# Seven-product gate and up for the last twelve tiles of two more FFN halves, with RWKV emitted at 2.5 steps

## The chip, the cores and the metric

The kernel runs on one core of one Trainium2 chip. The metric is the device time of one execution in microseconds; before the change it is 2428.38 us, the median of three runs (2426.93 to 2428.75). Five engines work side by side, each through its own instructions in a fixed order: TensorE (PE, with its weight loads PEld), VectorE (DVE), ScalarE (ACT), GpSimd (POOL) and SyncE (SP), which here issues the DMAs. [...]

## The reference

A decoder trunk on a sequence of 1024 tokens of width 1024, in float32. Two layers, each a mixer and a SwiGLU FFN with residual additions, and a final RMSNorm. Layer 0 mixes with causal pooling and a Mamba-2 SSD, layer 1 with RWKV-7 and an RG-LRU.

```python
for layer in range(DEPTH):                      # DEPTH = 2
    hn = rmsnorm(h, mix_norm_g[layer])
    h = h + (even_mixer if layer % 2 == 0 else odd_mixer)(hn, ...)
    hn = rmsnorm(h, ffn_norm_g[layer])
    h = h + swiglu(hn, ffn_w_gate[layer], ffn_w_up[layer], ffn_w_down[layer])
return rmsnorm(h, final_norm_g)

def swiglu(h, w_gate, w_up, w_down):            # 1024 -> 2816 -> 1024
    return (silu(h @ w_gate) * (h @ w_up)) @ w_down
```

RWKV is a recurrence over the tokens; the kernel computes it in chunks of 64 tokens, each of which needs the state that the chunk before it leaves.

## The kernel before

**Layout.** Activations lie transposed, features on the 128 partitions and tokens along the free axis. The tokens are worked in two halves of 512, so there are four FFN calls: (half, layer) = (0,0), (1,0), (0,1), (1,1). Every matrix product takes three matmuls for one (high part by high part, high by low, low by high, lines 370 to 372): each weight block arrives by DMA as a `raw` tile, ACT rounds it to its high part `whi` (line 348), DVE subtracts that to get the low part `wlo` (line 349), and so for the activations.

**Plain FFN.** `ffn` (line 478) works on pairs of 128-wide tiles of the 2816 hidden features: 22 tiles, 11 pairs. `gate_up` runs gate and then up through `dense`, with 48 matmuls of 512 columns for each tile; `down` multiplies a group of pairs by the down weights and adds into `h`. `GROUPS` gives the groups. `dense` yields after each block of four k tiles, 24 matmuls; such a stretch is called a main step below. A plain FFN has 72 of them, some with half the matmuls.

**Seven-product FFN.** The last call, (1,1), uses `stras_ffn` (line 667). For each tile the eight block products of gate and up with the token halves are replaced by seven (Strassen-Winograd): 84 matmuls of 256 columns, lines 663 to 665. It needs sums of the activations (`t1` to `t4`, made in `stras_norm`, line 590, from the normalized tiles, 16 persistent tiles of the tag `m`) and sums of the weights, which `stras_weights` (line 622) makes on DVE for every tile, with the splits into high and low. Four finished tiles are multiplied by the down weights in `down`.

**Order of the work.** The program is emitted by Python generators. `Side` and `weave` put RWKV (`rwkv`, about 63 steps) beside the FFN that does not depend on it: after each main step `RATES["rw"]` = 1.4 RWKV steps are emitted. The framework's scheduler then orders the instructions of each engine: earlier emission has the higher priority, and an instruction that is not ready is passed by later ones that are. On the engine that order is fixed. Buffers are tagged: a pool has a number of buffers for each tag, `m` has 28 (`BUFS`), `raw` 3, `whi` and `wlo` 4 each, `m4` 2. RWKV's 512-column tiles are all of the tag `m`.

In layer 1 the order is: FFN (1,0) with RWKV of half 0 beside it; `outproj` of half 0, and the input projection `in1` of half 1; FFN (0,1) with RWKV of half 1, where the weave stops at main step `LIMIT` = 58 to let `outproj` of half 1 run, with `stras_norm` inside the last pair; then the pool `oq` is closed, `sp` opened, and FFN (1,1) runs in seven products.

**Lines that the prediction follows.** RWKV first makes its per-chunk operands (lines 1203 to 1332: decays, scaled keys, `ps_A` products in line 1305, a triangular inverse `X` in lines 1327 and 1329, with trips through DRAM), then the chain of eight chunks: `chain1` (line 1408, matmul with the state `S`), an ACT copy (1410), `chain2` (1418), a DVE copy (1419), `chain3` (1429), two DVE operations that make the next state (1434, 1435). `gn` normalizes every second chunk (lines 1481 to 1508); its last tile is `ro`, line 1508. RWKV's output goes to DRAM and is read by `outproj`.

Of the kernel before, what the change touches and what calls it, by code (L numbers as in the profile page):

```python
# [5 lines left out]
F32 = mybir.dt.float32  # L6
# [80 lines left out]
class Trunk:  # L87
# [390 lines left out]
    def ffn(self, hf, layer, h, hn, nxt=None, r=None):  # L478
# [48 lines left out]

        pair = 0
# [61 lines left out]
    def stras_norm(self, X, h, r, gname, goff):  # L590


        nc = self.nc
        for k in range(4):
            f, s = [], []
            for j in (k, k + 4):
                hn = self.dp.tile([P, H], F32, name="hn", tag="tf", bufs=BUFS["tf"])
                nc.vector.scalar_tensor_tensor(hn, h[j], self.pv(gname, goff + j), r(), op0=MULT, op1=MULT)
                hl = self.hn_tiles(j)
                self.split(hn, *hl)  # L600
                f.append(hn)
                s.append(hl)
                if j < 4:
                    yield
            (b11, b12), (b21, b22) = [(x[:, :256], x[:, 256:]) for x in f]
            lo = [self.op.tile([P, H], F32R, name="tl", tag="m", bufs=BUFS["m"]) for _ in range(2)]
            hi = [self.op.tile([P, H], F32R, name="th", tag="m", bufs=BUFS["m"]) for _ in range(2)]
            ts = [self.m2("ts") for _ in range(2)]
            t1, t2, t3, t4 = [x[:, q * 256:(q + 1) * 256] for x in ts for q in range(2)]
            nc.vector.tensor_tensor(t1, b12, b11, op=SUB)  # L610
            nc.vector.tensor_tensor(t2, b22, t1, op=SUB)
            nc.vector.tensor_tensor(t3, b22, b12, op=SUB)
            nc.vector.tensor_tensor(t4, b21, t2, op=SUB)
            for q in range(2):
                self.split(ts[q], hi[q], lo[q])
            L, R = slice(0, 256), slice(256, 512)
            for b, (x, c) in dict(b11=(s[0], L), b21=(s[1], L), b22=(s[1], R), t1=((hi[0], lo[0]), L), t2=((hi[0], lo[0]), R),
                                  t3=((hi[1], lo[1]), L), t4=((hi[1], lo[1]), R)).items():
                X.setdefault(b, []).append([y[:, c] for y in x])
            yield  # L620

    def stras_weights(self, f, wg, wu):
# [16 lines left out]
        def one(src, pool, tag, bufs):  # L639
            hl = [pool.tile([P, 512], F32R, name=x, tag=tag, bufs=bufs) for x in ("wbh", "wbl")]  # L640
            self.split(src, *hl)
            return hl
# [3 lines left out]
        W["a22"] = one(a22, *((self.dp, "nrb", 2) if f % 2 else (self.dp, "h", BUFS["h"])))  # L646
# [5 lines left out]
        W["s2"] = one(a11, self.op, "m", BUFS["m"])  # L652
        nc.vector.tensor_tensor(a12, a12, a11, op=SUB)
        W["s4"] = one(a12, self.op, "m", BUFS["m"])
# [12 lines left out]
    def stras_ffn(self, hf, layer, h, X):  # L667
# [4 lines left out]
        acts = []  # L672

        def finish(e):
# [5 lines left out]
            if n % 8 < 5:  # L680
                hl = self.act_tiles()
            else:
                hl = [self.dp.tile([P, H], F32R, name=x, tag="h", bufs=BUFS["h"]) for x in ("acth", "actl")]
# [3 lines left out]
        def down(base, act):  # L687
            for m in range(4):
                pp = [self.psum("py"), self.psum("py")]
                for _ in self.dense(wd, base, len(act), m * 256, 256, act, pp):  # L690
                    pass
                for t in range(2):
                    nc.vector.tensor_tensor(h[2 * m + t], h[2 * m + t], pp[t], op=ADD)
                yield

        prev = None
        todo = None
        for n in range(NFF):
            W = self.stras_weights(n, wg, wu)
            Y, Z = self.pd("py1"), self.pd("pz1")  # L700
            self.stras_mm(Y[:, L], W["a11"], X["b11"], True)
            rr = self.dp.tile([P, H], F32, name="rr", tag="st", bufs=BUFS["st"])
            nc.scalar.copy(rr[:, L], Y[:, L])
            self.stras_mm(Z[:, R], W["s1"], X["t1"], True)
            c22 = self.dp.tile([P, H], F32, name="c22", tag="tf", bufs=BUFS["tf"])[:, :256]
            nc.scalar.copy(c22, Z[:, R])
            if prev:
                finish(prev)
            self.stras_mm(Y[:, L], W["s2"], X["t2"], False)
            nc.scalar.copy(rr[:, R], Y[:, L])  # L710
            self.stras_mm(Z[:, L], W["a12"], X["b21"], False)
            self.stras_mm(Z[:, R], W["s4"], X["b22"], False)
            g = self.dp.tile([P, H], F32, name="sg", tag="sg", bufs=BUFS["sg"])
            nc.vector.tensor_tensor(g, rr, Z, op=ADD)
            th = self.dp.tile([P, H], F32, name="th", tag="tf", bufs=BUFS["tf"])
            nc.scalar.activation(th, g, AF.Tanh, scale=0.5)
            nc.vector.scalar_tensor_tensor(g, th, 1.0, g, op0=ADD, op1=MULT)
            self.stras_mm(Y[:, L], W["s3"], X["t3"], False)
            nc.vector.tensor_tensor(c22, c22, Y[:, L], op=ADD)
            prev = (Y, W, g, c22, n)  # L720
            yield
            if n % 4 == 0 and n:
                todo = down(n - 4, acts[-4:])
            if todo:
                next(todo)
                yield
        finish(prev)
        yield from todo
        yield from self.ffn_final(hf, wd, NFF - 2, acts[-2:], h)
# [842 lines left out]
RATES = dict(o0=0.5, b0=4, ssd0=1.75, ssd1=1.0, rw=1.4)  # L1572
LIMIT = 58


def trunk(tc, ins, out):
    with ExitStack() as stack:
# [42 lines left out]
        with tc.tile_pool(name="op", bufs=1) as op, ExitStack() as late:  # L1620
            t.odd_open(op, late.enter_context(tc.tile_pool(name="oq", bufs=1)))
# [3 lines left out]
            side = Side(t.rwkv(0, sA))  # L1625
            st = weave(t.ffn(1, 0, hB, hn2), side, RATES["rw"])
            side.finish()
# [12 lines left out]
            side = Side(t.rwkv(1, sB))  # L1640
            hB = []
            hn = []
            X = {}
            f = t.ffn(0, 1, hA, hn2, t.stras_norm(X, hB, lambda: R["B"], "ffn_norm_g", 8))
            weave(f, side, RATES["rw"], LIMIT)
            side.finish()
            stB = run_all(t.outproj(1, 1, wo1, t.yd[1], hB, t.hn2, lambda: t.m2("hB")))
            t.later(2, lambda: rstd("B", stB))
# [33 lines left out]
```

## Time and profile before

| what | value |
|---|---|
| median of three runs | 2428.38 us |
| the profiled execution, device time | 2427.69 us |
| its span, first to last instruction | 2425.9 us |
| PE, PEld, DVE busy | 2373.9, 1986.4, 1656.8 us |
| ACT, POOL busy | 966.5, 244.0 us |
| mean granted TensorE clock | 0.992 of full speed |
| first gate matmul of FFN (1,0) | 909.0 us |
| first matmul of `outproj` of half 0 in layer 1 | 1370.0 us |
| first matmul of FFN (1,1) | 2068.7 us |

The shares are of the whole span; what a change in one stage is worth is read from that stage. A matmul's duration in the profile includes its way through the pipeline, so that consecutive ones overlap: the pace of a stream is read from how many start in a window, not from the mean duration.

### The profile page before, as it was taken

How to read it: one execution, taken by the hardware profiler on the slowest of the kernel's cores; microseconds unless marked ns; L12 is line 12 of the kernel's file. 1: busy time of each engine (PE TensorE's matmuls, PEld its weight loads, DVE VectorE, ACT ScalarE, POOL GpSimd, SP SyncE). 2: the span in 40 equal slices, each digit the busy share in tenths (PEclk: the TensorE clock that was granted, in tenths of full speed). 3: DMA queues.
4: the chain of work that ended last, by engine and by line, in shares of the span. 5: the costliest groups of instructions: out<-in, count | busy, mean ns of one | idle time of the engine just before them, and what ended most of it. 6: DMA issues, size and time to landing. Idle time of an engine off the chain costs nothing.

```text
span 2425.9 us, 34902 instructions
## 1 busy us (share of the span) xinstructions
PE 2373.9 (98%) x13115; PEld 1986.4 (82%) x13115; DVE 1656.8 (68%) x3248; ACT 966.5 (40%) x1708; POOL 244.0 (10%) x231
## 2 busy tenths in 40 slices
PE   7989999999999999999999999999999999899998
PEld 6878887888878887788888888877888887899997
DVE  7878767764476675775565668676656548887775
ACT  4444433322234555233333346442333334454442
POOL 2131121211112010100000111010000000000000
PEclk9999999999999999999999999999999999899999
DMA  5433533333245333644324443335433442333332
GB/s 165 120 91 103 158 112 103 89 111 98 83 135 178 88 117 88 167 132 123 99 78 141 145 133 94 109 114 158 136 103 91 117 140 83 122 113 105 103 103 73
DMA packets 318874, 280.28 MB, mean 116 GB/s; under 512 B 46067, under 2 KB 296073, under 8 KB 318705
## 3 DMA queue, kind: packets, MB, share of 16 engines
q1 hardware_dynamic: 317872, 277.64, 39.0%
q8 instruction: 103, 1.69, 0.3%
q0 software_dynamic: 832, 0.41, 0.1%
q14 instruction: 67, 0.54, 0.1%
HBM read 247.51 MB, written 30.49 MB: 115 GB/s over the span
## 4 chain that ended last, share of the span: by engine, by line
PE 91%; DVE 4%; DMA 2%; issue 1%; SPq 1%; ACT 1%; POOL 0%; DVEq 0%; ACTq 0%; POOLq 0%
PE py L370 6%; PE py L371 6%; PE py L372 6%; PE pg L371 5%; PE pg L372 5%; PE pg L370 5%; PE pu L370 5%; PE pu L371 5%; PE pu L372 5%; PE pi L370 4%; PE pi L371 4%; PE pi L372 4%; PE po L370 2%; PE po L371 2%; PE po L372 2%; PE py L663 2%
## 5 line engine op out<-in xcount | busy, mean ns | idle before, releaser
L348 ACT CAST whi<-raw 128x512 fp32r<-128x512 f32 (+1 forms) x664 | 407.6, 619 | 877.8 <-PE pu L371 207.9
L349 DVE TENSOR_TENSOR wlo<-raw,whi 128x512 fp32r<-128x512 f32 (+1 forms) x664 | 477.6, 723 | 401.5 <-ACT whi L348 394.7
L371 PE MATMUL py<-actl,whi 128*128 128x512 f32 x672 | 266.8, 397 | 0.0
L370 PE MATMUL py<-acth,whi 128*128 128x512 f32 x672 | 264.0, 401 | 1.4 <-DVE sg L510 0.5
L372 PE MATMUL py<-acth,wlo 128*128 128x512 f32 x672 | 264.9, 395 | 0.0
L370 PE MATMUL pu<-hnh,whi 128*128 128x512 f32 x560 | 223.5, 400 | 0.0
L371 PE MATMUL pu<-hnl,whi 128*128 128x512 f32 x560 | 223.1, 398 | 0.0
L372 PE MATMUL pu<-hnh,wlo 128*128 128x512 f32 x560 | 222.2, 397 | 0.0
L370 PE MATMUL pg<-hnh,whi 128*128 128x512 f32 x528 | 211.2, 400 | 0.0
L371 PE MATMUL pg<-hnl,whi 128*128 128x512 f32 x528 | 209.3, 396 | 0.0
L372 PE MATMUL pg<-hnh,wlo 128*128 128x512 f32 x528 | 208.4, 396 | 0.0
L370 PE MATMUL pi<-hnh,whi 128*128 128x512 f32 x512 | 204.4, 399 | 0.1
L371 PE MATMUL pi<-hnl,whi 128*128 128x512 f32 x512 | 203.2, 397 | 0.0
L372 PE MATMUL pi<-hnh,wlo 128*128 128x512 f32 x512 | 201.7, 396 | 0.0
L370 PEld LDWEIGHTS py<-acth,whi 128*128 128x128 f32 x672 | 126.9, 189 | 31.3 <-issue 1.5
L372 PEld LDWEIGHTS py<-acth,wlo 128*128 128x128 f32 x672 | 127.1, 189 | 29.1
L371 PEld LDWEIGHTS py<-actl,whi 128*128 128x128 f32 x672 | 127.1, 189 | 27.3 <-DVE actl L236 0.2
L522 DVE TENSOR_TENSOR h<-h,py 128x512 f32<-128x512 f32 x160 | 107.6, 682 | 34.9 <-PE py L372 33.8
L370 PEld LDWEIGHTS pu<-hnh,whi 128*128 128x128 f32 x560 | 105.3, 188 | 25.4 <-issue 2.2
L372 PEld LDWEIGHTS pu<-hnh,wlo 128*128 128x128 f32 x560 | 105.4, 188 | 24.4 <-issue 0.7
L371 PEld LDWEIGHTS pu<-hnl,whi 128*128 128x128 f32 x560 | 105.2, 188 | 24.4
L371 PEld LDWEIGHTS pg<-hnl,whi 128*128 128x128 f32 x528 | 99.3, 188 | 23.1
(499 smaller groups left out, 4862.9 us busy)
## 6 DMA issues: line engine op xcount, KB each, us to landing
raw<-in_ffn_w_gate SPq DMA_DIRECT2D x88, 512.0 KB
raw<-in_ffn_w_up SPq DMA_DIRECT2D x88, 512.0 KB
raw<-in_ffn_w_down SPq DMA_DIRECT2D x68, 512.0 KB
raw<-in_od_w_in SPq DMA_DIRECT2D x44, 512.0 KB
raw<-in_ev_w_in SPq DMA_DIRECT2D x36, 512.0 KB
raw<-in_ffn_w_down SPq DMA_DIRECT2D x40, 256.0 KB
yraw<-yd SPq DMA_DIRECT2D x32, 256.0 KB
raw<-in_ev_w_out SPq DMA_DIRECT2D x16, 512.0 KB
```

Of the source, the lines that this page charges most:

```text
L348: nc.scalar.copy(hi[:, :m, :width], raw[:, k:k + m, :width])
L349: nc.vector.tensor_tensor(lo[:, :m, :width], raw[:, k:k + m, :width], hi[:, :m, :width].bitcast(F32), op=SUB)
L370: nc.tensor.matmul(o, wh[:, a:b], xh, start=st, stop=False)
L371: nc.tensor.matmul(o, wh[:, a:b], xl, start=False, stop=False)
L372: nc.tensor.matmul(o, wl[:, a:b], xh, start=False, stop=en)
L522: nc.vector.tensor_tensor(h[f], h[f], pp[t], op=ADD)
L663: mm(o, ah[:, c], bh, start=first and k == 0, stop=False, skip_group_check=True)
```

## The change

Four things are changed together.

1. FFN (1,0) and FFN (0,1) run their first ten tiles plain, in groups of 2, 2 and 1 pairs (`PLAIN`), and their last twelve in seven products. `stras_ffn` is made general for it: a first tile `f0`, a list of group sizes ((4, 4, 4) and (2, 4, 4, 2); all 22 tiles of FFN (1,1) as before), a source of extra buffers, and two generators, one for the tiles and one for the downs that are left. `stras_late` makes the sums of the activations for them.
2. RWKV is woven at 2.5 steps for each main step, over 27 of the 32 plain main steps; what is left of it is then emitted at once, and the five last plain steps with `stras_late` after that.
3. For FFN (0,1), `outproj` of half 1 is emitted after all 22 tiles and ahead of the downs of the last two groups (`hold`); those downs, with `stras_norm` beside the first four of their steps, follow it.
4. Buffers: the pool `sp` is open for the whole of layer 1, with 4 instead of 6 buffers of the tag `ws`; every third pair of these comes from RWKV's tag `m4`. The split of `a22` moves from the tags `nrb` and `h` to `whi` and `wlo`, which the down weights use too. The scratch for DMA descriptors is set to 2048 bytes.

```diff
-    def ffn(self, hf, layer, h, hn, nxt=None, r=None):
+    def ffn(self, hf, layer, h, hn, nxt=None, r=None, groups=None):
...
+        if groups:
+            pair = 0
+            for ng in groups:
+                act = []
+                for _ in range(ng):
+                    yield from gate_up(pair, act)
+                    pair += 1
+                yield from down(2 * (pair - ng), act, False)
+            return None
...
+    def stras_late(self, X, hn):
+
+        for k in range(4):
+            s = [hn[k], hn[k + 4]]
+            f = [self.m2("tn") for _ in range(2)]
             for q in range(2):
-                self.split(ts[q], hi[q], lo[q])
...
+                self.nc.vector.tensor_tensor(f[q], s[q][0].bitcast(F32), s[q][1].bitcast(F32), op=ADD)
+            self.stras_sums(X, f, s)
             yield
...
         def two(src):
-            hi, lo = [self.sp.tile([P, 1024], F32R, name=x, tag="ws", bufs=6) for x in ("wah", "wal")]
+            pool, tag, bufs = (self.sp, "ws", 4) if self.nw % 3 else (self.oq, "m4", 2)
+            self.nw += 1
+            hi, lo = [pool.tile([P, 1024], F32R, name=x, tag=tag, bufs=bufs) for x in ("wah", "wal")]
...
-        W["a22"] = one(a22, *((self.dp, "nrb", 2) if f % 2 else (self.dp, "h", BUFS["h"])))
+        W["a22"] = one(a22, True)
...
+                    if todo and not (hold and gi == len(groups) - 1):
+                        next(todo, None)
+                        yield
...
-RATES = dict(o0=0.5, b0=4, ssd0=1.75, ssd1=1.0, rw=1.4)
-LIMIT = 58
+RATES = dict(o0=0.5, b0=4, ssd0=1.75, ssd1=1.0, rw=2.5)
+PLAIN = (2, 2, 1)
...
+            def beside(hf, layer, h, hn, side):
+
+                X = {}
+                f = t.ffn(hf, layer, h, hn, groups=PLAIN)
+                weave(f, side, RATES["rw"], 27)
+                side.finish()
+                g = t.stras_late(X, hn)
+                for _ in f:
+                    next(g, None)
+                run_all(g)
+                return X
+
+            X = beside(1, 0, hB, hn2, Side(t.rwkv(0, sA)))
+            g, f = t.stras_ffn(1, 0, hB, X, 10, (4, 4, 4), mm)
+            run_all(g)
+            st = run_all(f)
...
+            X = beside(0, 1, hA, hn2, Side(t.rwkv(1, sB)))
+            g, f = t.stras_ffn(0, 1, hA, X, 10, (2, 4, 4, 2), mm, True)
+            run_all(g)
             hB = []
-            hn = []
+            stB = run_all(t.outproj(1, 1, wo1, t.yd[1], hB, t.hn2, lambda: t.m2("hB")))
+            rstd("B", stB)
             X = {}
...
+            g = t.stras_norm(X, hB, lambda: R["B"], "ffn_norm_g", 8)
+            n = 0
+            for _ in f:
+                n += 1
+                if n < 5:
+                    next(g)
+                    next(g)
+            g, f = t.stras_ffn(1, 1, hB, X, 0, (4, 4, 4, 4, 4, 2),
+                               lambda: t.dp.tile([P, H], F32R, name="acte", tag="h", bufs=BUFS["h"]))
+            run_all(g)
             run_all(f)
             t.flush()
-            late.close()
-            with tc.tile_pool(name="sp", bufs=1) as t.sp:
-                run_all(t.stras_ffn(1, 1, hB, X))
```

More of the change, by code (lines that the diff above doesn't have):

```diff
@@ L604, in stras_norm @@
                     yield
[L605 to L610, printed above, removed]
@@ L672, in stras_ffn @@
         acts = []
+        ends = [f0 + sum(groups[:k]) for k in range(len(groups) + 1)]
+        left = []
+        st = self.Stat(self)
         def finish(e):
@@ L679, in finish, with down @@
             nc.vector.scalar_tensor_tensor(g[:, R], g[:, R], 0.5, c22, op0=MULT, op1=MULT)
-            if n % 8 < 5:
+            if (n - f0) % 8 < 5:
                 hl = self.act_tiles()
             else:
-                hl = [self.dp.tile([P, H], F32R, name=x, tag="h", bufs=BUFS["h"]) for x in ("acth", "actl")]
+                hl = [extra() for _ in range(2)]
             self.split(g, *hl)
             acts.append(hl)
-        def down(base, act):
+        def down(gi, last=False):
+            act = acts[ends[gi] - f0:ends[gi + 1] - f0]
@@ L688, in down @@
             for m in range(4):
                 pp = [self.psum("py"), self.psum("py")]
-                for _ in self.dense(wd, base, len(act), m * 256, 256, act, pp):
+                for _ in self.dense(wd, ends[gi], len(act), m * 256, 256, act, pp):
                     pass
                 for t in range(2):
-                    nc.vector.tensor_tensor(h[2 * m + t], h[2 * m + t], pp[t], op=ADD)
-                yield
[L696 to L726, printed above, removed]
@@ L732, in outproj, with rest @@
+        def rest():
+            if left[0]:
+                yield from left[0]
+            if layer == 1:
+                yield from self.ffn_final(hf, wd, ends[-2], acts[-2:], h)
+            else:
+                yield from down(len(groups) - 1, True)
+            return st
+        return tiles(), rest()
     def outproj(self, hf, layer, w, ydram, h, hnalloc=None, halloc=None):
@@ L1624, in trunk @@
             t.flush()
[L1625 to L1627 removed]
+            mm = lambda: op.tile([P, H], F32R, name="acte", tag="m", bufs=BUFS["m"])
+            def beside(hf, layer, h, hn, side):
[12 more added lines that the diff above has]
+            st = run_all(f)
             t.later(2, lambda: rstd("B", st))
```

94 lines of the change are left out of this document (70 added, 24 removed).

## The prediction

> **What bounds the kernel now.** First the page: the span, the engines, and the chain that ended last.
>
> ```profile
> span 2425.9 us, 34902 instructions
> PE 2373.9 (98%) x13115; PEld 1986.4 (82%) x13115; DVE 1656.8 (68%) x3248; ACT 966.5 (40%) x1708; POOL 244.0 (10%) x231
> ...
> PE 91%; DVE 4%; DMA 2%; issue 1%; SPq 1%; ACT 1%; POOL 0%; DVEq 0%; ACTq 0%; POOLq 0%
> ```
>
> TensorE is busy for 98% of the span and makes 91% of the chain. So fewer matmul cycles shorten the kernel as long as TensorE stays fed; whatever makes it wait is paid in full. The sum below is made against the profiled execution, 2427.69 us (span 2425.9 and 1.8 around it), which is 0.7 us under the median.
>
> The pace of the two kinds of tile comes from the view of busy time by window (window; its length; then for PE, PEld, DVE, ACT, POOL the busy time and in brackets how many started; granted clock, DMA share, GB/s). The first window lies in a plain FFN after RWKV is done, the second in the seven-product FFN.
>
> ```profile
> 1325.00:1350.00 25.00, 25.00 (x109) 20.19 (x108) 10.24 (x16) 8.13 (x14) 0.00 (x0) 1.00 0.21 64
> 2075.00:2100.00 25.00, 25.00 (x213) 24.95 (x211) 21.48 (x38) 13.39 (x22) 0.00 (x0) 1.00 0.42 127
> ```
>
> A 512-column matmul starts every 25/109 = 0.2294 us, a 256-column one every 25/213 = 0.1174 us. A plain tile's 48 take 11.01 us, a seven-product tile's 84 take 9.86 us: 1.15 us saved for each tile, not an eighth, because the short matmuls pay more for each column. DVE goes from 41% to 86% of the window.
>
> Next, how RWKV lies beside the plain FFN. From the views by tile: first gate matmul of FFN (1,0), first output-projection matmul after it (minimum, median, maximum ns, first and last start).
>
> ```profile
> L370 PE MATMUL pg<-hnh,whi x42: 387/394/481, 909.0 to 999.6; 128*128 128x512 f32 x42
> ...
> L370 PE MATMUL po<-yh,whi x128: 388/394/486, 1370.0 to 2001.2; 128*128 128x512 f32 x128
> ```
>
> The stage takes 461 us. How much of the plain work was done when RWKV's chain of chunks begins is counted by line 371 alone, one of three matmuls of every product (windows, PE and PEld only).
>
> ```profile
> 909.00:1098.50 189.50, 90.72 (x227) 43.07 (x227) 0.99 0.47 133
> ...
> 909.00:1284.00 375.00, 162.05 (x405) 76.55 (x405) 1.00 0.40 114
> ...
> 1546.50:1737.70 191.20, 90.66 (x228) 42.97 (x227) 0.99 0.47 132
> ```
>
> The first `chain1` runs at 1098.5. It is RWKV's 30th step, emitted at 1.4 after 22 main steps; but 227/8 = 28.4 main steps have been executed by then, 6 more than were emitted ahead of it. So from its second part on **RWKV runs behind its emission**: DVE operations, trips through DRAM and waits pace it, not the rate. The second stage shows the same (228). And 240 of line 371 are all that the ten plain tiles have (20 gate and up steps and 8 down steps of 8 each, 4 down steps of 4). When the chain begins, 13 are left: 13 x 3 x 0.2294 = 8.9 us. Now they last to the end of RWKV at 1284, where 405 were done.
>
> **The change part by part.**
>
> *Seven products for 24 tiles*: 24 x 1.15 = -27.6 us, 13.8 a stage. The downs keep their matmuls.
>
> *RWKV without cover.* The rate of 2.5 brings forward only what now waits for emission, the first six steps: the sixth comes after main step 3 instead of 5, 2 x 5.5 = 11 us; I take 10. The part before the chain then takes 179.5 us and leaves 18.9 us of plain work. One chunk, from the timeline of all engines (start, duration, engine, line):
>
> ```profile
> 1121.01 1.89 PE L1408 MATMUL ps_g<-S,w 128*128 128x64 f32 x16
> ...
> 1122.94 0.58 ACT L1410 COPY g<-ps_g 64x512 f32<-64x512 f32 x1 [2.04 <-PE ps_g L1408]
> ...
> 1127.88 1.14 PE L1418 MATMUL ps_u<-g,tt 64*64 64x64 f32 x16
> ...
> 1129.06 0.69 DVE L1419 COPY uv<-ps_u 64x512 f32<-64x512 f32 x1 [0.39 <-PE ps_u L1418]
> ...
> 1134.67 1.15 PE L1429 MATMUL ps_S<-uv,bk 128*64 128x64 f32 x16
> ...
> 1135.85 0.68 DVE L1434 TENSOR_TENSOR S<-S,ps_S 64x512 f32<-64x512 f32 x1 [1.32 <-PE ps_S L1429]
> ...
> 1136.56 0.68 DVE L1435 TENSOR_TENSOR S<-S,eld 64x512 f32<-64x512 f32 x1
> ...
> 1142.63 0.55 PE L1408 MATMUL ps_g<-S,w 128*128 128x64 f32 x4
> ```
>
> The period is 21.6 us, though the links add to 6.81 us: at 1123.5 `g` is ready, and `chain2` stands behind plain matmuls until 1127.88. RWKV's own TensorE time follows from the counts: 375 - 189.5 = 185.5 us, less (405 - 227) x 3 x 0.2294 = 122.5, is 63 us, 7.9 a chunk. A chunk without plain work therefore takes at least 7.9 us and at most 21.6; I take 9.0, near the links and the 7.9, the nearest rows. The 18.9 us cover 18.9/13.7 = 1.4 chunks at 21.6; 6.6 follow at 9.0: 89.6 us for the chain.
>
> After the last chunk `gn` and `ro` remain:
>
> ```profile
> 1266.40 0.58 ACT L1439 COPY ytm<-ps_g 64x512 f32<-64x512 f32 x1 [2.92 <-PE ps_g L1438]
> ...
> 1283.31 1.13 DVE L1508 SCALAR_TENSOR_TENSOR ro<-ps_yT,par,gg 128x128 f32<-128x128 f32 x4 [1.19 <-PE ps_yT L1504]
> ```
>
> That is 16.9 us with plain work in between; bounds 0 and 17, taken at half, 8.5.
>
> *The sums of `stras_late`.* They need `m` buffers, and I read the scheduler as giving a tag's buffers in the order of emission; RWKV's last, `ro`, comes ahead of them. Without that rule there is little room either: the chain holds 14 of 28 (8 `kb`, 4 `v`, `gd`, `gup`), two chunks in flight 10, two pairs of `ytm` and `vtm` 4. For each k: two adds of 512 columns, four differences of 256, two splits.
>
> ```profile
> L236 DVE TENSOR_TENSOR tl<-ts,th x8: 680/682/685, 2027.5 to 2060.5; 128x512 fp32r<-128x512 f32 x8
> L610 DVE TENSOR_TENSOR ts<-hn x4: 416/416/417, 2022.4 to 2053.8; 128x256 f32<-128x256 f32 x4
> ...
> L648 DVE TENSOR_TENSOR raw<-raw 128x512 f32<-128x512 f32 x22 | 15.1, 686 | 0.2
> ```
>
> 2 x 0.686 + 4 x 0.416 + 2 x 0.682 = 4.40 us, 17.6 for four, with `ro` and a hand-off 19.0. Until the second product of the first tile has all four, TensorE has only two tiles' first product, 24 x 0.1174 = 2.8 us.
>
> The sums are ready 179.5 + 89.6 + 8.5 + 19.0 = 296.6 us after the stage begins. TensorE's work until then: 189.5 + 8.9 + 63 + 2.8 = 264.2 us. **Idle: 32.4 us a stage.** How a stream restarts after such a pause is seen where FFN (1,1) begins (timeline of PE, then the window):
>
> ```profile
> 2068.68 0.55 PE L663 MATMUL py<-hnh,wah 128*128 128x256 f32 x1 [10.96 <-DVE xo L583]
> ...
> 2074.58 0.32 PE L663 MATMUL py<-hnh,wah 128*128 128x256 f32 x1
> ...
> 2050.00:2075.00 25.00, 14.04 (x97) 13.86 (x97) 22.47 (x65) 12.35 (x28) 0.00 (x0) 0.73 0.31 98
> ```
>
> After 10.96 us of waiting 27 matmuls take 5.90 us instead of 3.17: 2.7 us more. So 35.1 - 13.8 = +21.3 us a stage, **+42.6 us** for both.
>
> [...]
>
> *The start of FFN (1,1).* Those 10.96 us lie behind a full DVE (22.47 of 25 us), which held `xo` and so the PSUM buffers. `outproj` ahead of the held downs gives the norm 22 us of downs and 19 of `ffn_final` as cover instead of the last pair, but the same DVE work stands there. The wait may go (-13.7 with the restart) or grow by what plain work no longer covers, 11 us; I take 0. `outproj`'s 16 `m` tiles wait for the sums of the last tile, half free 48 matmuls (5.6 us) before its end; its 24 loads go through SP behind the last weights. Bound 0 to 5.6, taken at 0: four k tiles are 5.5 us of matmuls.
>
> *Buffers.* In the seven-product FFN DVE is nearly full, and `a22` now shares `whi` and `wlo` with the downs.
>
> ```profile
> 2125.00:2150.00 25.00, 25.00 (x178) 23.38 (x177) 22.81 (x37) 13.42 (x23) 0.00 (x0) 1.00 0.44 131
> ...
> L348 ACT CAST whi<-raw 128x512 fp32r<-128x512 f32 (+1 forms) x664 | 407.6, 619 | 877.8 <-PE pu L371 207.9
> L349 DVE TENSOR_TENSOR wlo<-raw,whi 128x512 fp32r<-128x512 f32 (+1 forms) x664 | 477.6, 723 | 401.5 <-ACT whi L348 394.7
> ...
> q0 software_dynamic: 832, 0.41, 0.1%
> ```
>
> Two of four are left for a down's block; if its split (0.62 + 0.72 us) were exposed in each of the 44 down steps beside such tiles, 59 us. I take 0, since 9.86 us of another tile lie between two down steps. The smaller descriptor scratch concerns POOL's queue with 0.1% of the DMA time: 0.
>
> Sum: 2427.7 - 27.6 + 2 x 35.1 = **2470 us**.
>
> **The rivals.** (1) *All is covered, and it is faster.* If the sums get `m` buffers earlier, or the chain is done before the plain work, no idle remains: 2400 us. It decides from 13.8 us of idle a stage down, that is, when the sums are ready by 275 us after the stage's start instead of 297. For it: RWKV's chain is only 6.8 us of links a chunk. Against it: the count of 227 of 240, and that the part before the chain can hardly shrink by 22 us, with DVE full in stretches of it (24.95 of 25 us):
>
> ```profile
> 975.00:1000.00 25.00, 24.63 (x118) 19.65 (x117) 24.95 (x52) 7.49 (x14) 8.04 (x7) 1.00 0.54 152
> ```
>
> (2) *It cancels*, 14 us of idle a stage: 2428. (3) *The chain runs cold or with its present hops.* Without dense matmuls between them the small ones may run at the slow pace seen at 2068: 7.9 x 0.2185/0.1174 = 14.7 us a chunk, 6.6 x 5.7 = 38 us more a stage: 2545. Exposed splits of the downs would lead to the same region. (4) *The rate does nothing*: that is part of the forecast.
>
> **How the numbers follow.** Forecast 0.53 (2440 to 2500: chunk 7.9 to 11 us, tail 0 to 17, start of FFN (1,1) -14 to +11), rival 1 0.32 (2388 to 2420), rival 2 0.05, rival 3 0.10. Within 0.2%, 5 us, a measurement of this kernel can't tell from no change. Faster 0.32, same 0.05, slower 0.63. Range 2398 to 2520: it takes in most of rival 1 and the forecast with its bounds, and leaves out the best of the one and most of rival 3.
>
> **What would show it.** In the changed profile: line 371 about 240 times before the second or third `chain1`; then chunks of about 9 us with TensorE under nine tenths; a gap of some 20 us ahead of the first matmuls that read `t1`, with DVE on lines of `stras_late` and `stras_sums`; 25-us windows of seven-product tiles with some 180 to 213 matmuls. The forecast is wrong if TensorE stays full between the last plain matmul and the first seven-product tile, if chunks stay at 21 us, or if `stras_late`'s sums run beside the chain.

## The result, and the profile after

The changed kernel takes 2518.39 us (median of four, 2511.98 to 2523.41); the kernel before took 2428.57 us beside it. The ratio is 1.0369, 95% interval 1.0344 to 1.0394: 90 us slower, where 43 were forecast. The direction was forecast, the size was not.

The page of the changed kernel's profile, its span, the engines, and the clock granted to TensorE in forty slices:

```profile
span 2515.5 us, 36915 instructions
PE 2410.3 (96%) x13979; PEld 2067.3 (82%) x13979; DVE 1804.8 (72%) x3496; ACT 1039.3 (41%) x1820; POOL 247.5 (10%) x231
PEclk9989999999999999996799999999968999999999
```

TensorE's busy time has grown by 36 us although it does less: there are two dips of the clock, and they lie where RWKV runs beside the two FFN halves that were changed. How long the plain work lasts beside RWKV is again counted by line 371 (windows of that line alone: window, length, busy time and count of PE, clock, DMA share, GB/s).

```profile
908.80:1086.36 177.56, 81.63 (x202) 0.98 0.46 131
...
908.80:1127.20 218.40, 96.91 (x240) 0.98 0.44 124
908.80:1250.00 341.20, 96.91 (x240) 0.87 0.36 101
```

The stage begins at 908.8, the first `chain1` at 1086.36, and at the third, 1127.2, all 240 are done. From there TensorE has the chain alone. The windows of all of PE from that point:

```profile
1125.00:1150.00 25.00, 23.12 (x189) 0.64 0.23 68
1150.00:1175.00 25.00, 24.83 (x228) 0.61 0.31 76
1175.00:1200.00 25.00, 22.39 (x228) 0.80 0.13 35
1200.00:1225.00 25.00, 7.41 (x25) 0.58 0.04 10
1225.00:1250.00 25.00, 22.37 (x159) 0.81 0.34 98
1250.00:1275.00 25.00, 25.00 (x196) 1.00 0.39 114
```

Two different things are to be seen. For 75 us TensorE is busy for 94% of the time, but its clock stands at 0.6 to 0.8. Then for 25 us it hardly works. The second is the forecast gap; its parts in the timeline of PE (in brackets the idle time before, and what ended it):

```profile
1209.64 1.08 PE L1557 MATMUL ps_yT<-cst,ytm 128*128 128x128 f32 x4 [9.89 <-DVE ytm L1545]
1214.88 0.58 PE L693 MATMUL pz<-th,wah 128*128 128x256 f32 x1 [4.15 <-ACT th L235]
...
1223.31 0.58 PE L693 MATMUL pz<-th,wah 128*128 128x256 f32 x1 [2.67 <-ACT th L235]
...
1227.49 0.58 PE L693 MATMUL pz<-th,wah 128*128 128x256 f32 x1 [2.67 <-ACT th L235]
```

First `gn` of the last pair, then one wait for each k of `stras_late`. On DVE the first sum follows right behind `ro`, as the order of the `m` buffers had it, and the waits for them end 4.2 us apart:

```profile
1210.84 1.13 DVE L1561 SCALAR_TENSOR_TENSOR ro<-ps_yT,par,gg 128x128 f32<-128x128 f32 x4 [1.35 <-PE ps_yT L1557]
1211.88 1.28 DVE L623 TENSOR_TENSOR tn<-hnh,hnl 128x512 f32<-128x512 f32 x2
...
1227.47 1.29 DVE L236 TENSOR_TENSOR tl<-ts,th 128x512 fp32r<-128x512 f32 x2 [0.22 <-ACT th L235]
```

So that gap was well read. The first, the slow clock, is where the forecast failed. An account of the whole loss shows it. From the first matmul of FFN (1,0) to the end of the span, in windows of 5 us, *idle* is the window less PE's busy time, and the *loss to the clock* is the busy time times (1 - granted clock). What is left is the work at full clock.

| profiled run | length | idle | loss to the clock | the rest |
|---|---|---|---|---|
| before | 1516.9 | 24.2 | 6.5 | 1486.2 |
| after | 1606.7 | 79.4 | 74.3 | 1453.0 |
| difference | +89.8 | +55.2 | +67.8 | -33.2 |
| forecast | +42.6 | +64.8 | +5.4 | -27.6 |

(The forecast's row is its own sum: twice 32.4 us of idle, twice 2.7 for a cold restart, 24 tiles at 1.15.) Work and idle time are about right; the clock is not.

### The profile page after: what moved, and what is told of

It is laid out like the page before. It is cut to its first block, busy times and chain, and to the rows that moved or that the text cites. A ratio compares the mean times of both kernels' runs of the same rounds, so it can differ in the third digit from the quotient of the medians.

```text
span 2515.5 us, 36915 instructions
## 1 busy us (share of the span) xinstructions
PE 2410.3 (96%) x13979; PEld 2067.3 (82%) x13979; DVE 1804.8 (72%) x3496; ACT 1039.3 (41%) x1820; POOL 247.5 (10%) x231
## 5 line engine op out<-in xcount | busy, mean ns | idle before, releaser
L370 PE MATMUL pu<-hnh,whi 128*128 128x512 f32 x368 | 147.5, 402 | 0.0
L371 PE MATMUL pu<-hnl,whi 128*128 128x512 f32 x368 | 146.6, 398 | 0.0
L235 ACT CAST wah<-raw 128x1024 fp32r<-128x1024 f32 x92 | 96.2, 1049 | 110.5 <-DMA raw<-in_ffn_w_gate 51.6
L370 PE MATMUL pg<-hnh,whi 128*128 128x512 f32 x336 | 134.9, 401 | 0.0
L371 PE MATMUL pg<-hnl,whi 128*128 128x512 f32 x336 | 133.6, 398 | 0.0
L372 PE MATMUL pg<-hnh,wlo 128*128 128x512 f32 x336 | 132.3, 394 | 0.0
L236 DVE TENSOR_TENSOR wal<-raw,wah 128x1024 fp32r<-128x1024 f32 x92 | 112.4, 1221 | 25.1 <-ACT wah L235 22.2
L370 PEld LDWEIGHTS pi<-hnh,whi 128*128 128x128 f32 x512 | 96.8, 189 | 24.4 <-issue 1.2
L372 PEld LDWEIGHTS pi<-hnh,wlo 128*128 128x128 f32 x512 | 96.6, 189 | 22.6
L371 PEld LDWEIGHTS pi<-hnl,whi 128*128 128x128 f32 x512 | 96.7, 189 | 22.5 <-issue 0.6
```

The lines of the kernel that those rows point to most:

```text
L235: nc.scalar.copy(hi, src)
L236: nc.vector.tensor_tensor(lo, src, hi.bitcast(F32), op=SUB)
L370: nc.tensor.matmul(o, wh[:, a:b], xh, start=st, stop=False)
L371: nc.tensor.matmul(o, wh[:, a:b], xl, start=False, stop=False)
L372: nc.tensor.matmul(o, wl[:, a:b], xh, start=False, stop=en)
```

## The experiments

Each ran beside the kernel before on the same chip; its ratio is to those runs. On that scale the changed kernel stands at 1.0369.

**The rate alone.** The changed kernel with `RATES["rw"]` as it was.

```diff
-RATES = dict(o0=0.5, b0=4, ssd0=1.75, ssd1=1.0, rw=2.5)
+RATES = dict(o0=0.5, b0=4, ssd0=1.75, ssd1=1.0, rw=1.4)
```

> The changed kernel with RWKV's rate back at 1.4 steps a yield, all else as changed. Theory (the loss comes from chunks of RWKV's chain that stand without plain matmuls, because only ten tiles are plain, and from the sums behind them): the plain work runs out at the same place, so within 12 us of the changed kernel, 2506 to 2530 us. Rival (the rate of 2.5 does the harm, by pushing RWKV ahead of dense work): 2450 us or less.

2511.2 us, ratio 1.0357 (1.0336 to 1.0377): the rate does nothing that can be told from zero. The first `chain1` comes at 1097.3 instead of 1086.4, as before the change, and the rest takes as much less.

**More plain tiles.**

```diff
-PLAIN = (2, 2, 1)
+PLAIN = (2, 2, 2, 2)
...
-            g, f = t.stras_ffn(1, 0, hB, X, 10, (4, 4, 4), mm)
+            g, f = t.stras_ffn(1, 0, hB, X, 16, (4, 2), mm)
...
-            g, f = t.stras_ffn(0, 1, hA, X, 10, (2, 4, 4, 2), mm, True)
+            g, f = t.stras_ffn(0, 1, hA, X, 16, (2, 4), mm, True)
```

> The changed kernel with 16 plain tiles and 6 of seven products beside RWKV in both stages instead of 10 and 12. Theory: six more plain tiles put 6 x 11 us of dense matmuls beside the chain, all chunks but the last one or two are covered, the gap ahead of the first seven-product tile shrinks below 10 us a stage, so nearly all of the 90 us of loss goes: 2415 to 2440 us. Rival (the seven-product tiles themselves, or what follows them, cost the time): half the tiles bring back half of the loss, about 2475 us.

2466.8 us, ratio 1.0173 (1.0158 to 1.0189). The last group of the second stage has four tiles here, and `ffn_final` takes two: the downs of the other two, 2 x 24 matmuls or 11 us, are left out, so the like figure is some 2478. The expectation was missed, and its rival's reason doesn't hold either, as the PE windows show:

```profile
1250.00:1275.00 25.00, 22.41 (x108) 1.00 0.26 75
1275.00:1300.00 25.00, 14.54 (x68) 0.59 0.15 43
```

Up to 1271 every chunk is covered and the clock is at 1.00. But covered chunks take 21.6 us each, as before the change, so RWKV ends together with the plain work, and the sums stand bare behind it just the same. Cover does not help a thing that comes after it.

**The sums earlier.** They are emitted between RWKV's steps 55 and 63.

```diff
-                weave(f, side, RATES["rw"], 27)
-                side.finish()
-                g = t.stras_late(X, hn)
-                for _ in f:
-                    next(g, None)
-                run_all(g)
+                weave(f, side, RATES["rw"], 22)
+                g = t.stras_late(X, hn)
+                for _ in range(4):
+                    next(g)
+                    next(f)
+                    side.step(2)
+                run_all(g)
+                side.finish()
+                run_all(f)
```

> The changed kernel with the four groups of sums emitted between RWKV's steps 55 and 63 instead of behind its last one. Theory: the sums take m buffers that RWKV has set free by then and run on VectorE beside the last two chunks; the waits of 10 + 4 + 6 us ahead of and in the first seven-product tile go and its matmuls fill the last chunk, less some delay of the chain: 18 to 25 us a stage, 2470 to 2485 us. Rival (the sums aren't what the tile waits for, or they delay the chain by as much on VectorE): 2510 us or more.

2512.1 us, ratio 1.0371 (1.0351 to 1.0390): no gain. The idle time did fall (59.9 us instead of 79.4), but the loss to the clock rose from 74.3 to 84.3. DVE now has the sums, the norm, the weight splits of the first seven-product tiles and the chain's copies at once, and the last two chunks of the first stage take 16.1 and 15.2 us instead of 13.2 and 9.0. The rival was right here.

**Filling the chain.** Three 512-column matmuls that nobody reads behind each of three places of a bare chunk (one without plain matmuls beside it).

```diff
+        def dense_fill(c):
+            if c >= 2:
+                d = self.psum("ps_d")
+                for q in range(3):
+                    nc.tensor.matmul(d, self.fill[q][0][:, :P], self.fill[q][0], start=True, stop=True)
...
             chain1(c)
+            dense_fill(c)
             yield
...
             chain2(c)
+            dense_fill(c)
             yield
...
             chain3(c)
+            dense_fill(c)
...
+                t.fill = hn
```

> The changed kernel with three 128x512 matmuls, read by nobody, behind each of three places of chunks 2 to 7 of the chain: 54 a stage, 12.4 us of TensorE at full clock. Theory (an uncovered chunk is TensorE's own work at about half clock, and the clock falls because the small matmuls come with short waits between them): the granted clock stays above 0.9 there, a chunk takes 8 + 2.1 = 10 us instead of 13 to 15, 12 to 17 us a stage are saved: 2484 to 2494 us, although work is added. Rival A (the hand-offs between engines set 13 us a chunk at any clock): the added matmuls lie in waits, within 8 us of the changed kernel. Rival B (the clock stays at half whatever is added): 13 + 4 us a chunk, 2550 us or more.

2518.4 us, ratio 1.0385 (1.0365 to 1.0404): as the changed kernel, with 108 matmuls more (24.8 us at 0.2294 us each; by the account the rest grew by 37). The windows that stood at 0.64 and 0.61:

```profile
1125.00:1150.00 25.00, 23.31 (x216) 0.93 0.24 68
1150.00:1175.00 25.00, 22.71 (x241) 0.93 0.29 78
```

The clock came up, the loss to it fell from 74.3 to 33.8 us, and the fill cost what that gave. So the number of rival A came about by another way than rival A's. A second thing showed: in every second bare chunk of the first stage TensorE waited 1.6 to 2.2 us for `ytm`, the norm's output, and the clock fell behind that wait, to 0.72, 0.83 and 0.50 in the windows of 5 us from 1143.58, 1168.58 and 1193.58. So the norm holds TensorE up through its own output.

**Without the sums.** t1 to t4 are halves of the plain input; the real sums are left out.

```diff
     def stras_late(self, X, hn):
...
-            self.stras_sums(X, f, s)
+            for b, (x, c) in dict(b11=(s[0], L), b21=(s[1], L), b22=(s[1], R), t1=(s[0], L), t2=(s[0], R),
+                                  t3=(s[1], L), t4=(s[1], R)).items():
+                X.setdefault(b, []).append([y[:, c] for y in x])
```

> The changed kernel without the sums for its seven-product tiles beside RWKV: the products b12-b11 and so on are taken from plain halves of the input instead (t1 to t4 are left out, 4 x 4.4 us of VectorE and ScalarE a stage). Theory: in the changed kernel TensorE stands 9.9 + 4.2 + 0.7 + 2.7 + 2.7 = 20 us a stage at the end of RWKV and comes back cold, because the sums wait for RWKV's last tiles; without them the first seven-product tile runs beside the last chunk and the norm, 15 to 22 us a stage: 2474 to 2488 us. The rest of the loss, about 22 us a stage, stays: chunks at half clock. Rival (VectorE's other work there, the norm and the weight splits, fills the same time): 2505 us or more.

2480.1 us, ratio 1.0223 (1.0202 to 1.0245): 35 us for two stages, as the theory had it. The sums are some 18 us a stage; the larger part of the loss is elsewhere.

**Both kernels without RWKV.** Its inputs are written to its output rows, and all of its arithmetic is left out.

```diff
     def rwkv(self, hf, st):
...
         for j in range(4):
+            self.nc.sync.dma_start(self.yd[hf][j * P:(j + 1) * P, :], st["r"][j])
+            yield
```

> The changed kernel with the whole of RWKV left out (its four input tiles are written to its output rows instead). Theory: nothing is left that has to be covered, the sums run beside plain tiles, and the changed kernel is below the kernel before without RWKV by the price of the products, 24 x 1.15 = 27.6 us less the start of the last FFN and some waits at the hand-over: 18 to 28 us. Rival (the seven-product tiles cost time themselves, by VectorE or by shared buffers): no less than the other, or slower.

> The kernel before with the whole of RWKV left out in the same way. RWKV's own matmuls go, and nothing else changes: all theories expect about 120 us a stage or less off the kernel before, 2190 to 2330 us; it is there for the difference to the run above.

2227.1 and 2238.1 us: with nothing to cover the change is worth 11 us, less than the 18 to 28 expected. The engines' rows of the two pages, changed kernel first:

```profile
PE 2171.9 (98%) x11827; PEld 1862.8 (84%) x11827; DVE 1577.1 (71%) x2924; ACT 938.4 (42%) x1638; POOL 200.2 (9%) x178
```

```profile
PE 2189.0 (98%) x10963; PEld 1834.2 (82%) x10963; DVE 1435.9 (64%) x2676; ACT 867.3 (39%) x1526; POOL 198.9 (9%) x178
```

TensorE has 17 us less to do and DVE 141 us more, at 71% of the span. By the account above the work falls by 23.2 us, and idle time and the clock take back 12.2. Of these, 5.8 us lie behind the first matmul of the last output projection, where the last FFN begins; that start was forecast at 0. The other 6.4 lie ahead of it and are made of waits under 3 us.

**More plain tiles and earlier sums.** The edits of the second and third run together, with groups (4, 2) in both stages, so that nothing is left out.

> 16 plain and 6 seven-product tiles beside RWKV, the second stage's groups 4 and 2, and the sums emitted between RWKV's steps 55 and 63. Theory (both things that were lost are given back: plain matmuls beside every chunk, and sums that don't come behind RWKV): no long wait of TensorE at the end of RWKV, the clock at 1.0 there, and the six tiles' products show: each stage 461 - 6.9 = 454 us, and with 3 us more at the start of the last FFN 2412 to 2425 us. Rival (sums beside plain tiles delay the chain, or seven-product tiles don't pay): 2430 us or more.

2443.4 us, ratio 1.0076 (1.0061 to 1.0091). The best of the complete versions, but still 0.6 to 0.9% above the kernel before. The work falls by 10.0 us for twelve tiles, idle grows by 20.4 and the loss to the clock by 6.7. The longest wait at RWKV's end is 3.6 us; the idle time is made of many waits of 1 to 3 us, for `sg`, `wah`, `ytm` and `yh`, on DVE and ACT. The theory had not counted those, and the rival's number came out.

**The same cover, spread thin.** The work of the changed kernel and its order in the chain stay. The last 96 plain matmuls are held, so that four stand behind each of the chain's 24 hops (three groups of matmuls in each of eight chunks); before, 20 to 25 stood behind each hop of the first chunk and a half.

```diff
+    def held(self, x):
+        if self.hold is not None:
+            k = int(self.hold / self.per)
+            if k < len(self.hops):
+                self.after(self.hops[k], x)
+            self.hold += 1
...
-                    nc.tensor.matmul(o, wh[:, a:b], xh, start=st, stop=False)
+                    self.held(nc.tensor.matmul(o, wh[:, a:b], xh, start=st, stop=False))
...
-                weave(f, side, RATES["rw"], 27)
+                t.hops = []
+                weave(f, side, RATES["rw"], 26)
                 side.finish()
+                t.hold, t.per = 0, 4
```

> The changed kernel with the same work, and its last 96 plain matmuls a stage held so that four of them stand behind each of the 24 hops of RWKV's chain, instead of 20 to 25 behind each hop of the first one and a half chunks and none behind the rest. Theory (most of the loss is the clock: in the changed kernel TensorE's busy time at a lowered clock loses 33 and 41 us in the two parts, against 2 and 5 before, because the bare chunks cool it, and full cover is not needed to prevent that): chunks of 8 + 3 x 4 x 0.23 = 11 us at a clock above 0.9, the chain ends 15 to 20 us sooner, 2465 to 2485 us. Rival (a hop's waits set 13 us a chunk, or the clock falls anyway): 2505 us or more.

2507.0 us, ratio 1.0341 (1.0326 to 1.0357): 7 us by the ratios, inside the rival's bound. The loss to the clock fell from 74.3 to 48.5 us, but idle time rose from 79.4 to 89.7. Two of its waits, in PE's timeline:

```profile
1120.62 0.63 PE L1572 MATMUL ps_yT<-cst,ytm 128*128 128x128 f32 x4 [2.69 <-DVE ytm L1560]
...
1172.50 1.12 PE L1496 MATMUL ps_S<-uv,bk 128*64 128x64 f32 x16 [2.47 <-DVE uv L1486]
```

Both are for DVE. A chunk took 9 to 21 us. Four plain matmuls behind a hop, 0.92 us, do not cover such waits, and TensorE still slows behind the first of these: `ps_bk` takes 1.06 us at 1123.06 and 0.61 at 1135.04. What made the waits became the open question.

**Thin cover and earlier sums.** The edits of the third and of the last run together.

> The run above with the sums emitted between RWKV's steps 55 and 63 too. Theory: cover and sums are two separate losses that add up (leaving the sums out was worth 38 us on the changed kernel, emitting them early 6, since VectorE had the first tiles' weight splits to do at the same time): 10 to 30 us below the run above. Rival (VectorE is the limit at the end of RWKV and the order of its work doesn't matter): within 8 us of the run above.

2490.7 us, ratio 1.0280 (1.0252 to 1.0309): 15 us below the last run by the ratios, as the theory had it. Why the earlier sums pay here and not without the thin cover stays open.

**The same with twelve plain tiles.**

```diff
-PLAIN = (2, 2, 1)
+PLAIN = (2, 2, 2)
...
-            g, f = t.stras_ffn(1, 0, hB, X, 10, (4, 4, 4), mm)
+            g, f = t.stras_ffn(1, 0, hB, X, 12, (4, 4, 2), mm)
...
-            g, f = t.stras_ffn(0, 1, hA, X, 10, (2, 4, 4, 2), mm, True)
+            g, f = t.stras_ffn(0, 1, hA, X, 12, (4, 4, 2), mm, True)
...
-                t.hold, t.per = 0, 4
+                t.hold, t.per = 0, 5
```

> The run above with 12 plain and 10 seven-product tiles, five plain matmuls behind each hop, and some 70 plain matmuls left for the end of the chain. Theory: the two more plain tiles (33 us of dense work) stand beside the tail of 11 us and the sums of 18 us, so TensorE neither waits long nor cools there; ten tiles at 1.15 us gained are 11.5 us a stage: 2410 to 2430 us, at or below the kernel before. Rival (VectorE's load at the end of RWKV remains the limit): 2440 us or more.

2469.6 us, ratio 1.0187 (1.0168 to 1.0205): better again, but the theory's 2410 to 2430 are missed and the rival's bound holds. Idle time is still 62.8 us and the loss to the clock 23.4, against 24.2 and 6.5 before the change.

**Without the norm beside the chain.** By now three runs pointed at `ytm`. This one leaves out `part1` of the group norm for three of the four pairs.

```diff
-                gq += self.gn(hf, p, ch["y", p], ch["vtm", p], bon, gd)
+                gq += self.gn(hf, p, ch["y", p], ch["vtm", p], bon, gd)[0 if c == 7 else 1:]
```

> The changed kernel with the first part of RWKV's group norm (its sum, variance, root and scaling: some 20 VectorE instructions, 8 us, and a square on ScalarE) left out for three of the four pairs of chunks; the last pair and the second parts stay. Theory A (the norm on VectorE holds up the chain's copy of u, the waits of 1 to 1.4 us that follow cool the clock, and the chunk runs at half clock): all bare chunks take about 8 to 8.5 us at a clock above 0.9, 4 x 5 us a stage are saved, 2475 to 2485 us. Theory B (bare chunks of small matmuls cool the clock by themselves, norm or not): 12 us a chunk, 2505 us or more.

2472.7 us, ratio 1.0198 (1.0176 to 1.0219): 41 us by the ratios, and theory A's chunks to the letter. The starts of five bare chunks lie 7.7, 8.9, 7.4, 8.9 and 7.5 us apart (1124.8 to 1165.3), 8.1 on average; in the changed kernel the same five took 12.5 (1127.2 to 1189.7). By the account the gain is the clock's: the loss to it falls from 74.3 to 25.0 us, idle time only from 79.4 to 77.2. The run with the old rate says the same without leaving anything out. Over its two stages the third, fifth and seventh chunks, which have the norm's first part beside them, take 13.7 to 15.6 us, and the second, fourth and sixth 7.4 to 8.2, but for one of 12.8.

How the norm does it is seen in the first bare chunk of the changed kernel, on PE:

```profile
1127.22 1.90 PE L1461 MATMUL ps_g<-S,w 128*128 128x64 f32 x16
...
1129.87 1.11 PE L1471 MATMUL ps_u<-g,tt 64*64 64x64 f32 x16 [0.32 <-ACT g L1463]
1130.92 0.69 PE L1440 MATMUL ps_m<-xn,aoff 32*32 32x32 f32 x16
1132.45 1.94 PE L1482 MATMUL ps_S<-uv,bk 128*64 128x64 f32 x16 [0.85 <-DVE uv L1472]
1134.32 1.97 PE L1491 MATMUL ps_g<-uv,arb 64*64 64x64 f32 x16
...
1140.87 3.51 PE L1461 MATMUL ps_g<-S,w 128*128 128x64 f32 x16
```

and on DVE:

```profile
1127.22 1.22 DVE L236 TENSOR_TENSOR wal<-raw,wah 128x1024 fp32r<-128x1024 f32 x1
...
1128.96 1.22 DVE L236 TENSOR_TENSOR wal<-raw,wah 128x1024 fp32r<-128x1024 f32 x1
1130.09 0.68 DVE L1539 TENSOR_REDUCE gs<-gsq 128x8 f32<-128x512 f32 x1
1130.69 0.42 DVE L1436 STREAM_TRANSPOSE tt<-xn 32x256 f32<-32x256 f32 x1
1131.14 0.43 DVE L1437 STREAM_TRANSPOSE tt<-xn 32x256 f32<-32x256 f32 x1
1131.61 0.69 DVE L1472 COPY uv<-ps_u 64x512 f32<-64x512 f32 x1
```

`ps_u` is written at 1131.0, but the copy `uv` stands on DVE behind a split, the norm's reduction and two transposes. TensorE waits 0.85 us, 1.2 with the wait before, and from 1132.4 on every matmul takes nearly double: `ps_S` 1.94 us instead of 1.15, `ps_g` of the next chunk 3.51 instead of 1.90. Without the norm DVE is idle when `ps_u` comes (its row in the second bare chunk of this run, and PE's next one):

```profile
1136.53 0.69 DVE L1472 COPY uv<-ps_u 64x512 f32<-64x512 f32 x1 [2.65 <-PE ps_u L1471]
```

```profile
1137.28 1.15 PE L1482 MATMUL ps_S<-uv,bk 128*64 128x64 f32 x16 [0.17 <-DVE uv L1472]
...
1125.00:1150.00 25.00, 23.99 (x329) 1.00 0.40 113
```

The last line is the window: the same small matmuls, bare, at full clock. It is not their smallness alone that cools it.

The delayed copy is not the norm's only way. In the first bare chunk of the second stage TensorE has the same waits of 0.32 and 0.85 us, and the clock stays at 1.00; it falls at 1818.2, in a wait for `ytm`, the norm's own output:

```profile
1812.72 1.12 PE L1482 MATMUL ps_S<-uv,bk 128*64 128x64 f32 x16 [0.85 <-DVE uv L1472]
...
1818.70 1.09 PE L1557 MATMUL ps_yT<-cst,ytm 128*128 128x128 f32 x4 [2.08 <-DVE ytm L1545]
```

This run takes both away at once, so how much each of them costs is not shown.

**Without the norm and without the sums.** The edits of the runs without the sums and without the norm together, with both left out.

> The run above with the sums left out as well (t1 to t4 taken from plain halves of the input). If chunks and sums are the whole loss, the two add up: 38 us below the run above, 2435 to 2450 us, still above the kernel before by what is left of the tail and of the chunks, less the products' gain. If something else lies behind them (VectorE's weight splits, the hand-over to the last FFN), less than 25 us below the run above.

2444.6 us, ratio 1.0073 (1.0053 to 1.0093): in the range, and 30 us below the last run by the ratios instead of 38. Together the two make up 72 of the 90 us. Idle time and the loss to the clock add to 80.1 us, against 153.7 in the changed kernel and 30.7 before. Much of what is left in the first stage lies at the end of the chain, where the last pair's norm still stands: from 1165 to 1205 TensorE is busy for 30.66 of 40 us at a clock of 0.79, with waits of 1.94 us for `ytm` and 4.56 us for the split weights of a seven-product tile. No run takes these away.

**The held downs first.** The third part of the change is undone.

```diff
+            run_all(f)
             hB = []
             stB = run_all(t.outproj(1, 1, wo1, t.yd[1], hB, t.hn2, lambda: t.m2("hB")))
             rstd("B", stB)
             X = {}
-            g = t.stras_norm(X, hB, lambda: R["B"], "ffn_norm_g", 8)
-            n = 0
-            for _ in f:
...
+            run_all(t.stras_norm(X, hB, lambda: R["B"], "ffn_norm_g", 8))
```

> The changed kernel with its third part undone: the six held tiles' downs run ahead of the output projection, and the last FFN's sums are emitted behind it in one piece. Theory: the held downs (6 x 5.5 = 33 us of dense matmuls) cover the sum of squares, the eight norms and the sums of the last FFN; without them VectorE's 40 us for these stand bare: 20 to 40 us slower than the changed kernel, 2538 to 2558 us. Rival (they cover little, since the start waits for the sum of squares in any order): within 8 us of the changed kernel.

2526.5 us, ratio 1.0421 (1.0386 to 1.0456), with a wide spread (2517.9 to 2538.3). The interval touches that of the changed kernel: 8 us by the medians, 13 by the ratios, between the two theories' numbers. The order seems to help a little, and it is no part of the loss.

## Why the prediction was right in direction and wrong in size

**The products.** Forecast 27.6 us less work. The account gives 33.2 beside RWKV, 23.2 without it: right within what such an account can tell. A window that shows the new tiles (1250 to 1275, quoted above) has 196 matmuls and a full clock, inside the forecast's 180 to 213; later windows go down to 168. TensorE is busy for 25.00 of 25 us in each window from 1250 to 1375, so no exposed splits of the downs are seen: the shared `whi` and `wlo` cost nothing large.

**The start of the chain.** Forecast 179.5 us after the stage's start with 18.9 us of plain work left. It came after 177.6, with (240 - 202) x 3 x 0.2294 = 26.2 us left. Right but for 7 us of cover; the rate has no effect beyond those 10 us, and the run with the old rate shows that even these are not worth anything at the end.

**The chunks: the step that failed.** The text took the links of 6.81 us and TensorE's own 7.9, and "I take 9.0", with 21.6 as the upper bound. The chain was to last 89.6 us. It lasted 112.3 (1086.4 to the end of the last `chain3` at 1198.7): 22.7 us more in the first stage, which is the whole of the stage's miss (43.5 us lost instead of 21.3). In the second stage it lasted 114.4. The sign named for it, TensorE under nine tenths, did not come either: it was busy for 94%, at a lowered clock. Two things were left out of the 9.0. The links were read from a chunk in which DVE was free when `ps_u` came; `gn`'s `part1` was put into the tail alone, although it stands on DVE beside every second chunk, some 19 instructions long, and TensorE waits for its output too (2.08 us before 1818.70). And the clock: the forecast had 2.7 us a stage for it, and the loss was 34 (67.8 over both). Without the norm a bare chunk takes 8.1 us at full clock (1.00 in every window of 5 us from 1125 to 1165), so the 9.0 would have been high: the reading of links and TensorE's own work was right, and what delays the links was missed.

The first two chunks also kept a full cover of 22.2 and 18.6 us instead of 1.4 chunks of 21.6.

**The cold chain as a rival.** Rival 3 had 14.7 us a chunk and a chance of 0.10, with "the slow pace seen at 2068" as its price. Measured were 12.5 on average: 12.8 to 14.8 with the clock at half for all or part of the chunk, 8.0 where it had come back. So the cold chain came, but not for the rival's reason: without the norm the same small matmuls, with nothing dense between them, kept the full clock in those windows. The two should have shared the weight the other way round, since the trace of before had already shown TensorE at nearly half pace behind a wait (10.96 us of waiting, then 27 matmuls in 5.90 us instead of 3.17). That the measured 2518 us lies inside the range of 2398 to 2520 is luck: the range was meant to leave out most of this rival.

**Tail and sums.** Forecast 8.5 + 19.0 = 27.5 us behind the last chunk. From 1198.7 to the last split at 1228.8 it is 30.1. Right, and the rows fit the rule that the `m` buffers come in the order of emission, though no run tests it: the first `tn` stands directly behind `ro`. Leaving the sums out was worth some 18 us a stage; the theory's forecast of 17.6 for them was right.

**The idle time.** Forecast 64.8 us more, measured 55.2: less, since the chain, slow at a lowered clock, kept TensorE busy (24.83 of 25 us at 0.61 from 1150 on).

**The start of the last FFN.** Taken at 0 between -13.7 and +11. The wait of 10.96 us went, and waits of 2.78 and 2.44 us for the sum of squares and several for weights came. From the first matmul of the last output projection to the end, idle time and loss to the clock are 26.0 us instead of 23.1: about 3 us, within the bounds (without RWKV 5.8).

**That no version beat the kernel before** has its reason in the pair without RWKV: with nothing in the way, twenty-four such tiles are worth 11 us here, while RWKV needs cover for its chain, its norm and, newly, the sums behind it. The plain tiles were that cover.

## What to carry to other kernels

When dense work that covers a dependent chain is made shorter, price the uncovered chain with everything that stands on the queues of its copies, not with its links alone; here the norm of 19 small VectorE instructions turned waits of 0.2 us into waits of 1 to 2, and these cost more through the clock than as waits: with its first part left out for three of the four pairs the loss to the clock fell by 49.3 us and idle time by 2.2. Keep three things apart in the account, work at full clock, idle time, and busy time at a lowered clock: here the first fell by 33 us as planned and the third rose by 68. And let what follows a chain, such as operands for the next stage, not wait for the chain's own buffers: cover beside the chain did nothing for sums that came behind it.

## What the runs showed of the hardware that was not expected

In the changed kernel the clock fell to 0.50 behind waits of at most 0.85 us, and then stayed there for 37.55 us while TensorE was busy. These are windows of PE, cut where the clock changes and 3.4 and 6.8 us ahead of it, around the first bare chunks of the two stages:

```profile
1128.73:1132.15 3.42, 2.55 (x40) 1.00 0.55 177
1132.15:1169.70 37.55, 36.54 (x283) 0.50 0.20 52
1169.70:1183.35 13.65, 11.84 (x164) 1.00 0.33 79
1183.35:1190.18 6.83, 6.83 (x56) 0.50 0.00 0
1190.18:1193.59 3.41, 2.69 (x32) 1.00 0.26 77
1193.59:1197.00 3.41, 3.41 (x20) 0.50 0.13 37
...
1811.40:1814.81 3.41, 2.56 (x47) 1.00 0.58 165
1814.81:1818.22 3.41, 1.80 (x26) 1.00 0.06 10
1818.22:1848.94 30.72, 30.24 (x229) 0.50 0.22 59
```

No wait around 1132.15 was longer than 0.85 us. Then TensorE was busy for 36.54 of 37.55 us, and the clock stood at 0.50 all that time.

In these rows the clock is either 1.00 or 0.50, and the stretches between its changes are 37.55, 13.65, 6.83, 3.41, 3.41 and 30.72 us long: within 0.04 us, 11, 4, 2, 1, 1 and 9 times the shortest. TensorE's busy time just ahead does not tell the fall: the rows that end at 1132.15 and at 1814.81 have 2.55 and 2.56 us of it, and the clock fell behind the first and not behind the second. What made the difference, and what ended the 37.55 us at half clock, is not shown.

In the run without the norm, waits of 0.17 to 0.32 us at one or two places of a chunk left the clock at 1.00 for the window from 1125 to 1150.
